# Half-width column sums, earlier decode states, later gate work and a longer last yield in a one-layer hybrid decoder step

## The chip, the core and the metric

The kernel runs on one core of one Trainium2 chip. A core has the matrix engine TensorE (PE), whose weight loads are listed apart as PEld, the vector engine VectorE (DVE), the scalar engine ScalarE (ACT), GpSimd (POOL), and SyncE (SP), which issues most of the DMAs. Each engine works through its own instructions in order and waits on semaphores for the others. The metric is the device time of one execution in microseconds (us), as the median of several runs.

## What is computed

One inference step of a one-layer decoder, for a prompt of 1024 positions and for 8 decode sequences of 4 positions, width 1024, all in float32. Two half-step feed-forward layers stand around a mixer of two groups of heads: a matrix-memory recurrence (mLSTM, 4 heads of 128) and sliding-window attention (SWA, 8 heads of 64).

```python
def half_ffn(x, j, gpre, gpost):
    y = swiglu(rmsnorm(x, g[gpre]), ffn_w_gate[l, j], ffn_w_up[l, j], ffn_w_down[l, j])
    return x + 0.5 * rmsnorm(y, g[gpost])

x = half_ffn(x, 0, 0, 1)
h = rmsnorm(x, g[2])
(qm, km, vm, om, ip, fp), (qa, ka, va) = split_proj(h, w_in[l], b_gate[l])
u_m, new_m = mlstm_heads(qm, km, vm, om, ip, fp, mstate, mlstm_norm_gain[l], h.dtype)
u_a, new_kv = swa_prompt(qa, ka, va, attn_sinks[l])      # swa_sample for the decode rows
u = jnp.concatenate([u_m, u_a], axis=-1)
x = x + rmsnorm(u @ w_out[l], g[3])
x = half_ffn(x, 1, 4, 5)
```

```python
def rmsnorm(x, g):
    y = xf * lax.rsqrt(jnp.mean(xf * xf, axis=-1, keepdims=True) + RMS_EPS)
    return (y * g.astype(jnp.float32)).astype(x.dtype)

def mlstm_chunk(carry, xs):                              # state C, n, m; gates ig, fg
    b = jnp.cumsum(jax.nn.log_sigmoid(fg), axis=-1)
    ...
    m_t = jnp.maximum(inter, jnp.max(D, axis=-1))        # running maximum
    num = a[..., None] * jnp.einsum('bhtk,bhkv->bhtv', q, C) + jnp.einsum('bhts,bhsv->bhtv', S, v)
    ...
    C_new = decay[..., None, None] * C + jnp.einsum('bhs,bhsk,bhsv->bhkv', wk, k, v)
```

The outputs are the new x of both parts, the last keys and values, and the new states C, n, m.

## The kernel before

The 1056 rows (1024 of the prompt, 32 of the decode sequences) are held transposed, features on the partitions, in four quarters of 264 columns (`QW`): 256 of the prompt and 8 of decode. Two blocks of 128 features, `kp` pairs, lie side by side in a tile of 128x528. Each float32 weight is split by ACT (`wh`, a cast, L196) and DVE (`wl`, the rest, L197), activations likewise, and a product is three matmuls (`wh` by high, `wl` by high, `wh` by low), all recorded at the line of the helper `pe`, L154.

There are three phases: 1 is the first feed-forward layer, 2 the mixer's output projection, 3 the second feed-forward layer. In a feed-forward layer `gu` are the gate and up matmuls and `pd` the down matmuls; in the mixer `pz` is the input projection and `po` the output projection.

**What sets the order.** The Python program emits instructions for all engines in one pass. `Order` keeps a clock `now`, advanced by an estimate for every matmul that `pe` emits. Side work is written as generators: `yield w` puts the rest of the generator off until `now` has moved on by `w` us of planned PE time. What is emitted between two yields goes into each engine's queue at that place, SP's DMAs and POOL's copies too; the engine keeps this order on the chip.

**After a product block** (`post`). `out_block` takes a `ps` of `pd` or `po` to the tile `y` and its square into `acc`, summed on DVE (L502). `col_stats` sums squares over the partitions with matmuls against a column of ones: for three windows of 128 columns (`WIN`, of which the third overlaps the second) and the two halves of the tile, six one-column matmuls into `cs`. `rstd` makes the reciprocal root of it on DVE (L260 to L271), a matmul (`rb`) spreads it over the partitions, ACT copies it (`cr`), DVE scales `y` (L443) and adds the residual `x` (L444). Where another layer follows, the new rows are squared (ACT L448), summed (DVE L452) and go through `col_stats` again. `post` yields `PW[0]` = 4.0 before the first sums and `PW[3]` = 6.0 before the second. Phase 3 ends with `store_y`: `yT`, transposes on PE (L151), copies (`yo`) and stores.

**The last quarter** has a class of its own, `Last`. `block(mo, ps)` runs for each of the eight row blocks `mo`; `first` and `second` turn `y` as it comes. `finish` computes the sums from two tiles, `acc[0]` (row blocks 0 to 6) and `acc[1]` (the last, squared at L545), with six matmuls, then scales and stores (L590 to L596).

**Gates** (`gate_rows`, `gates`). The gate rows are turned by PE into `gr`, copied by ACT to `H` and `lf` (L966), scanned by DVE (L992: four cumulative sums and then four running maxima for each of two groups), and then exponentials are formed by ACT into `G` (L996, L998, L999). Beside that runs attention: scores `sws`, their exponentials (ACT L1102), transposes `swp` on PE, a copy of these to `swpT` by ACT (L1136) or DVE (L1138), and the product `swo` on PE.

**Decode states** (`mlstm_sample`). For the 8 decode sequences, in pairs: load the state `Cb` (128x4x128; SP L1436), copy in the column of `n` (POOL L1437), 8 matmuls `sinter` of the queries with the old state, 8 matmuls `sU` of keys and values, DVE updates of the state (L1455), and the store `o_s_C` (SP L1460). Between the parts stand yields of `BW` = 2.4. The loads of a pair come right ahead of its matmuls. The weight loads of `w_out` (SP L1602, L1604) are on the same queue and wait until a raw buffer (`NRAW` = 2) has been read.

## Time and profile before

| | us |
|---|---|
| three runs of the kernel | 2036.6, 2038.76, 2040.52 |
| their median | 2038.76 |
| profiled execution, its own time | 2040.95 |
| span of its profile | 2039.1 |
| granted TensorE clock, mean | 0.988 |
| TensorE busy | 2007.4 |
| VectorE, ScalarE, GpSimd busy | 1165.4, 873.8, 34.1 |

The span runs from the first to the last instruction of the profile; the profiled execution took 1.85 us more. Busy shares are of the span. An arrow `<-` in a row joins what is written to what is read; behind the bar of a row of a group stand its busy time, the mean time of one in ns, and the idle time of the engine just ahead with what ended it. In a row of the timeline or the chain the first two numbers are the start and the length in us, and the square bracket is the idle time just ahead with its releaser. A matmul of float32 operands, as in `cs`, leaves two records, so the x12 of a chain piece are six matmuls.

### The profile page before, as it was taken

What the parts mean: (1) busy time and instruction counts of PE and PEld (TensorE: products, weight loads), DVE (VectorE), ACT (ScalarE), POOL (GpSimd) and SP (SyncE); (2) the same over time, 40 slices, a digit from 0 to 9 for tenths busy, and PEclk for the clock granted to TensorE, in tenths of its full rate; (3) what the DMA queues carried; (4) which work ended last, traced back from release to release, by engine and by line L of the source; (5) the groups of instructions that cost most, each with busy time, mean ns of one, the idle gap of its engine ahead of it and who ended that gap; (6) DMA issues with size and microseconds to landing.
All of it is one profiled execution on the core that took longest, in us unless ns stands there. A gap on an engine that the chain in (4) does not pass through costs nothing.

```text
span 2039.1 us, 40481 instructions
## 1 busy us (share of the span) xinstructions
PE 2007.4 (98%) x16244; PEld 1962.1 (96%) x16244; DVE 1165.4 (57%) x2811; ACT 873.8 (43%) x2087; POOL 34.1 (2%) x166
## 2 busy tenths in 40 slices
PE   7999999999999999999999999999999999999998
PEld 7999999999999999987998999999999999999998
DVE  6855555557248236467455757785555556533764
ACT  6533333336246232356252555353333334433553
POOL 0000000000000002000001000000000000000000
PEclk9999999999999999999998999999999999999999
DMA  6122222236256252101313234322222223544773
GB/s 234 65 81 87 83 64 83 85 100 176 87 161 203 86 147 87 49 1 38 75 52 101 75 108 134 117 64 90 68 75 82 89 70 118 166 132 153 215 233 115
DMA packets 279691, 216.68 MB, mean 106 GB/s; under 512 B 21032, under 2 KB 252640, under 8 KB 279488
## 3 DMA queue, kind: packets, MB, share of 16 engines
q1 hardware_dynamic: 279504, 214.11, 34.7%
q8 instruction: 127, 2.08, 0.4%
q14 instruction: 60, 0.49, 0.1%
HBM read 172.39 MB, written 42.49 MB: 105 GB/s over the span
## 4 chain that ended last, share of the span: by engine, by line
PE 91%; DMA 3%; DVE 3%; ACT 1%; issue 1%; SPq 0%; DVEq 0%; POOL 0%; ACTq 0%; POOLq 0%
PE gu L154 40%; PE pd L154 23%; PE pz L154 7%; PE pw L154 4%; PE pl L154 4%; PE pv L154 3%; PE po L154 3%; DMA raw<-ffn_w_down 2%; PE cs L154 1%; PE sws L154 1%; PE swo L154 1%; PE rb L154 1%; PE E L154 1%; PE swp L151 1%; ACT wh L196 0%
## 5 line engine op out<-in xcount | busy, mean ns | idle before, releaser
L154 PE MATMUL gu<-Xh,wh 128*128 128x264 f32 x2240 | 636.1, 284 | 1.2 <-ACT sc L736 1.2
L154 PE MATMUL gu<-Xl,wh 128*128 128x264 f32 x2240 | 636.2, 284 | 0.0
L154 PE MATMUL gu<-Xh,wl 128*128 128x264 f32 x2240 | 635.8, 284 | 0.0
L197 DVE TENSOR_TENSOR wl<-raw,wh 128x512 fp32r<-128x512 f32 x458 | 302.5, 670 | 390.4 <-ACT wh L196 383.6
L154 PE MATMUL pd<-hq,wh 128*128 128x264 f32 x2816 | 523.1, 287 | 0.0
L196 ACT CAST wh<-raw 128x512 fp32r<-128x512 f32 x458 | 270.5, 602 | 468.1 <-PE pd L154 200.3
L154 PEld LDWEIGHTS pd<-hq,wh 128*128 128x128 f32 x2816 | 439.4, 190 | 0.0
L154 PEld LDWEIGHTS gu<-Xh,wh 128*128 128x128 f32 x2240 | 421.3, 188 | 1.7 <-ACT sc L736 1.4
L154 PEld LDWEIGHTS gu<-Xh,wl 128*128 128x128 f32 x2240 | 421.6, 188 | 0.0
L154 PEld LDWEIGHTS gu<-Xl,wh 128*128 128x128 f32 x2240 | 421.3, 188 | 0.0
L154 PE MATMUL pd<-hq,wl 128*128 128x264 f32 x1408 | 401.7, 285 | 0.0
L154 PEld LDWEIGHTS pd<-hq,wl 128*128 128x128 f32 x1408 | 266.3, 189 | 0.0
L736 ACT COPY sc<-gu 128x264 f32<-128x264 f32 x240 | 90.8, 379 | 273.7 <-PE gu L154 270.6
L197 DVE TENSOR_TENSOR wl<-ws,wh 128x512 fp32r<-128x512 f32 x160 | 108.9, 690 | 87.3 <-ACT wh L196 84.4
L747 DVE TENSOR_TENSOR h<-gu,sc 128x264 f32<-128x264 f32 x120 | 51.8, 432 | 103.2 <-PE gu L154 83.4
L154 PE MATMUL pz<-xh,wh 128*128 128x264 f32 x352 | 103.5, 294 | 0.0
L154 PE MATMUL pz<-xl,wh 128*128 128x264 f32 x352 | 101.9, 289 | 0.0
L154 PE MATMUL pz<-xh,wl 128*128 128x264 f32 x352 | 101.2, 287 | 0.0
L196 ACT CAST wh<-ws 128x512 fp32r<-128x512 f32 x160 | 95.8, 622 | 3.7 <-PE pl L154 2.5
L748 ACT ACTIVATE h<-h 128x264 f32<-128x264 f32 x120 | 50.9, 425 | 106.7 <-DVE h L747 106.7
L753 DVE TENSOR_TENSOR sc<-gu,sc 128x264 f32<-128x264 f32 x120 | 51.6, 432 | 57.2 <-PE gu L154 51.6
L154 PE MATMUL pl<-Xl,wh 128*128 128x264 f32 x256 | 75.3, 298 | 1.0 <-DVE Xl L197 0.8
(367 smaller groups left out, 2997.0 us busy)
## 6 DMA issues: line engine op xcount, KB each, us to landing
raw<-ffn_w_down SPq DMA_DIRECT2D x80, 512.0 KB
raw<-ffn_w_gate SPq DMA_DIRECT2D x44, 512.0 KB
raw<-ffn_w_up SPq DMA_DIRECT2D x44, 512.0 KB
h<-h SPq DMA_DIRECT2D x80, 264.0 KB
hq<-h SPq DMA_DIRECT2D x160, 132.0 KB
raw<-ffn_w_down SPq DMA_DIRECT2D x40, 384.0 KB
x<-xs SPq DMA_DIRECT2D x48, 264.0 KB
raw<-w_in SPq DMA_DIRECT2D x21, 512.0 KB
```

The source lines that it names most:

```text
L151: K.nc.tensor.transpose(out, lhsT, rhs)
L154: K.nc.tensor.matmul(out, lhsT, rhs, start=start, stop=stop, **kw)
L196: K.nc.scalar.copy(hi, src)
L197: (eng or K.nc.vector).tensor_tensor(lo, src, hi.bitcast(F32), op=ALU.subtract)
L736: nc.scalar.copy(sc[n][:, g], ps)
L747: nc.vector.tensor_tensor(d, bk[tg, g], sc[n][:, g], op=ALU.add)
L748: nc.scalar.activation(d, d, AF.Silu)
L753: nc.vector.tensor_tensor(sc[n][:, g], src, sc[n][:, g], op=ALU.add)
```

## The change

Five edits:

1. `col_stats` gets the phase. In phases 1 and 3 DVE first adds the two halves of the sum tile (128x264, in place), and three matmuls follow in place of six. Phase 2 is as before.
2. In the last quarter the three sums of `acc[0]` are made in a task of their own, due 2.0 us after row block 6; the three of `acc[1]` remain in `finish`, and both write one `cs`.
3. In phase 3, `post` yields 2.0 once more before `store_y`.
4. `gate_rows` yields 1.5, 1.5 and 2.0 around its arithmetic, and `gates` yields 7.0 ahead of its exponentials.
5. `mlstm_sample` issues the loads of the first four states (and the POOL copies of their columns) at its start, and later those of the pair after the next.

```diff
@@ -235,12 +235,17 @@
         K.od.tick()
 
 
-def col_stats(K, acc):
+def col_stats(K, acc, phase):
 
     ps = sbank(K, "cs")
+    n = 2
+    if phase != 2:
+
+        K.nc.vector.tensor_tensor(acc[:, 0:QW], acc[:, 0:QW], acc[:, QW:2 * QW], op=ALU.add)
+        n = 1
     for j, w in enumerate(WIN):
-        for i in range(2):
-            pe(K, ps[:, j:j + 1], acc[:, i * QW + w:i * QW + w + P], K.ones, start=(i == 0), stop=(i == 1))
+        for i in range(n):
+            pe(K, ps[:, j:j + 1], acc[:, i * QW + w:i * QW + w + P], K.ones, start=(i == 0), stop=(i == n - 1))
     return ps[:, 0:3]
 
 
@@ -430,7 +435,7 @@
         nc.sync.dma_start(t, K.xs[q][kp])
         x.append(t)
     yield PW[0]
-    ss = col_stats(K, acc.pop())
+    ss = col_stats(K, acc.pop(), phase)
 
     c = rstd(K, ss, 4.0 / D, 4.0 * EPS) if half else rstd(K, ss)
     yield PW[1]
@@ -461,11 +466,12 @@
                 nc.vector.scalar_tensor_tensor(lo, y[kp][:, s], gk, hi.bitcast(F32), op0=ALU.mult, op1=ALU.subtract)
         yield PW[2] if q > 1 else PL[phase]
     if not nxt:
+        yield 2.0
         yield from store_y(K, q, y)
         return
     K.od.done.add(("x", phase, q))
     yield PW[3]
-    r = rstd(K, col_stats(K, acc))
+    r = rstd(K, col_stats(K, acc, phase))
     yield PW[4]
     if nxt == "mix":
         rc = K.kp.tile([P, 3], F32, tag=f"rc{q}", name=nm(K, "rc"), bufs=1)
@@ -548,10 +554,22 @@
         else:
             self.acc.append(sq)
         nc.scalar.activation(y, ps, AF.Copy, scale=gain)
+        if mo == 6:
+            K.od.spawn(self.stats(0), 2.0)
         if mo == 3:
             K.od.spawn(self.first(self.t), 3.0)
         elif mo > 3:
             K.od.spawn(self.second(mo, y), 3.0)
+
+    def stats(self, i):
+
+        if i == 0:
+            self.ss = sbank(self.K, "cs")
+        for j, w in enumerate(WIN):
+
+            pe(self.K, self.ss[:, j:j + 1], self.acc[i][:, w:w + P], self.K.ones, start=(i == j == 0),
+               stop=(i == 1 and j == 2), skip_group_check=True)
+        yield 0
 
     def first(self, t):
         K = self.K
@@ -576,13 +594,11 @@
 
     def finish(self):
         K, q = self.K, self.q
-        ps = sbank(K, "cs")
-        for j, w in enumerate(WIN):
-            for i, sq in enumerate(self.acc):
-                pe(K, ps[:, j:j + 1], sq[:, w:w + P], K.ones, start=(i == 0), stop=(i == 1))
+        for _ in self.stats(1):
+            pass
         K.od.drain()
 
-        c = rstd(K, ps[:, 0:3], 4.0 / D, 4.0 * EPS)
+        c = rstd(K, self.ss[:, 0:3], 4.0 / D, 4.0 * EPS)
         for j in range(3):
             for x in range(2):
                 o = tmp(K, "yo", 512)
@@ -946,12 +962,15 @@
     nc.gpsimd.tensor_copy(R[:, :, 0:4], v[:, :, 0:4])
     nc.scalar.activation(e, f, AF.Abs)
     nc.scalar.activation(e, e, AF.Exp, scale=-1.0)
+    yield 1.5
 
     nc.vector.tensor_scalar(u, e, 1.0, None, op0=ALU.add)
     nc.vector.scalar_tensor_tensor(d, u, 1.0, e, op0=ALU.subtract, op1=ALU.subtract)
     nc.vector.tensor_scalar(e, e, -0.5, 1.0, op0=ALU.mult, op1=ALU.add)
     nc.vector.tensor_tensor(d, d, e, op=ALU.mult)
+    yield 1.5
     nc.scalar.activation(u, u, AF.Ln)
+    yield 2.0
     nc.vector.tensor_tensor(u, u, d, op=ALU.subtract)
     nc.vector.scalar_tensor_tensor(R[:, :, 32:36], f, 0.0, u, op0=ALU.min, op1=ALU.subtract)
     yield 8.0
@@ -993,6 +1012,7 @@
         nc.vector.tensor_tensor(K.mst[:, c + 1:c + 2], b[:, o + P - 1:o + P], M[:, o + P - 1:o + P], op=ALU.add)
     nc.vector.tensor_scalar(p(I), p(M), -1.0, None, op0=ALU.mult)
     nc.vector.tensor_tensor(p(d), p(b), p(M), op=ALU.add)
+    yield 7.0
     nc.scalar.activation(p(G[64:68]), p(d), AF.Exp, scale=-1.0)
     for c, o in chunks:
         nc.scalar.activation(G[32:36, o:o + P], M[:, o:o + P], AF.Exp, bias=K.mst[:, c:c + 1], scale=-1.0)
@@ -1400,12 +1420,22 @@
 
     nc, A, O = K.nc, K.A, K.O
     c = 8
+    states = []
+
+    def state(b):
+        Cb = slot(K, "Cb")[:, 0:516].rearrange("p (h v) -> p h v", v=129)
+        nc.sync.dma_start(Cb[:, :, 0:P], A["state_mlstm_C"][0, b].rearrange("h k v -> k h v"))
+        nc.gpsimd.tensor_copy(Cb[:, :, P], n0[:, b])
+        states.append(Cb)
+
     nrow = tmp(K, "n0", P)[0:32]
     nc.sync.dma_start(nrow, A["state_mlstm_n"][0].rearrange("b h k -> (b h) k"))
     ps = bank(K, "n0T", "c")
     pe(K, ps[:, 0:32], nrow, K.ident[0:32, 0:32], tr=True)
     n0 = K.kp.tile([P, 8, 4], F32, tag="n0", name="n0", bufs=1)
     nc.vector.tensor_copy(n0.rearrange("p b h -> p (b h)"), ps[:, 0:32])
+    for b in range(4):
+        state(b)
     E = scores(K, c, [K.sz[:, 6 + h] for h in range(HM)], [K.sz[:, 10 + h] for h in range(HM)], K.H[2][0], 32, slot)
 
     kr = slot(K, "kr")[:, 0:512]
@@ -1430,12 +1460,10 @@
     nn = K.kp.tile([P, 8, 4], F32, tag="nn", name="nn", bufs=1)
     for b0 in range(0, 8, 2):
 
-        bs, C = (b0, b0 + 1), []
-        for b in bs:
-            Cb = slot(K, "Cb")[:, 0:516].rearrange("p (h v) -> p h v", v=129)
-            nc.sync.dma_start(Cb[:, :, 0:P], A["state_mlstm_C"][0, b].rearrange("h k v -> k h v"))
-            nc.gpsimd.tensor_copy(Cb[:, :, P], n0[:, b])
-            C.append(Cb)
+        bs = (b0, b0 + 1)
+        for b in range(len(states), min(b0 + 4, 8)):
+            state(b)
+        C = [states[b] for b in bs]
         for b, Cb in zip(bs, C):
             for h in range(HM):
                 q = qm[h // 2][:, (h % 2) * 256 + b * 32:(h % 2) * 256 + b * 32 + 32]
```

Three places where the order of the instructions moves. Numbers behind a name count tiles as the program makes them, and the same tile has another number in the changed kernel; its line numbers are shifted too.

SP, at the decode states (`raw` a buffer for `w_out` weights, `Cb` a state to be loaded, `o_s_C` the output of new states), before:

```order
L1602 DMA raw_13850<-w_out 128x4x128
L1604 DMA raw_13850<-w_out 64x4x128 x2
L1602 DMA raw_14144<-w_out 128x4x128
L1604 DMA raw_14144<-w_out 64x4x128 x2
L1436 DMA Cb_13686<-state_mlstm_C 128x4x128
L1436 DMA Cb_13689<-state_mlstm_C 128x4x128
L1436 DMA Cb_13751<-state_mlstm_C 128x4x128
L1436 DMA Cb_13754<-state_mlstm_C 128x4x128
L1460 DMA o_s_C<-Cb_13686 128x4x128
L1460 DMA o_s_C<-Cb_13689 128x4x128
L1460 DMA o_s_C<-Cb_13751 128x4x128
L1460 DMA o_s_C<-Cb_13754 128x4x128
```

SP at the same place after the change, where L1602, L1604, L1436 and L1460 are L1630, L1632, L1427 and L1488:

```order
L1630 DMA raw_13840<-w_out 128x4x128
L1632 DMA raw_13840<-w_out 64x4x128 x2
L1427 DMA Cb_13619<-state_mlstm_C 128x4x128
L1427 DMA Cb_13622<-state_mlstm_C 128x4x128
L1427 DMA Cb_13625<-state_mlstm_C 128x4x128
L1427 DMA Cb_13628<-state_mlstm_C 128x4x128
L1630 DMA raw_14128<-w_out 128x4x128
L1632 DMA raw_14128<-w_out 64x4x128 x2
L1488 DMA o_s_C<-Cb_13619 128x4x128
L1488 DMA o_s_C<-Cb_13622 128x4x128
L1427 DMA Cb_13741<-state_mlstm_C 128x4x128
L1427 DMA Cb_13744<-state_mlstm_C 128x4x128
```

The four state loads have moved ahead of the second `w_out` load; the loads of the third pair stand behind two stores, where before they stood behind the four that are shown.

ACT, at the gates of the first group (`H`, `lf` and `G` of the gates; `sws`, `es`, `swpT`, `kT` of attention), before:

```order
L1102 ACTIVATE sws_11477,den_11473<-sws_11477,nmx_11472 128x256 x2
L966 COPY H_11551<-gr_11546 4x2x256
L966 COPY lf_11552<-gr_11546 4x2x256
L998 ACTIVATE G_11556<-lf_11552,mst 4x128 x4
L1136 COPY swpT_11641<-swp_11636 128x512
L999 ACTIVATE G_11556<-G_11556,H_11551 4x128 x3
L996 ACTIVATE G_11556<-gb_11555 4x2x256
L999 ACTIVATE G_11556<-G_11556,H_11551 4x128
L1119 COPY kT_11676<-kT_11674 128x128
```

ACT after the change, from the same `swpT` copy on (L1136, L1102, L1099, L966 are L1156, L1122, L1119, L985):

```order
L1156 COPY swpT_11592<-swp_11587 128x512
L1119 ACTIVATE es_11539<-es_11539 128x4
L1122 ACTIVATE sws_11544,den_11541<-sws_11544,nmx_11540 128x256 x2
L1122 ACTIVATE sws_11545,den_11541<-sws_11545,nmx_11540 128x256 x2
L985 COPY H_11617<-gr_11612 4x2x256
L985 COPY lf_11618<-gr_11612 4x2x256
```

ACT after the change, the rows that follow directly (`z` takes up `swo`, `wh` is a weight cast, L998 is L1018):

```order
L1170 COPY z_9873<-swo_11502 128x128
L1139 COPY kT_11651<-kT_11649 128x128
L1170 COPY z_9937<-swo_11502 128x128
L1018 ACTIVATE G_11622<-lf_11618,mst 4x128 x2
L196 CAST wh_11785<-raw_11783 128x512
L1018 ACTIVATE G_11622<-lf_11618,mst 4x128
L1156 COPY swpT_11707<-swp_11702 128x512
L1018 ACTIVATE G_11622<-lf_11618,mst 4x128
```

The `swpT` copy that stood behind the four instructions of L998 now stands ahead of the copies to `H` and `lf`, and the next `swpT` copy stands behind three of the four.

DVE, at the third set of sums in phase 1 (`wl` a weight rest, `sq` squares, `xl` the rest of an activation), before:

```order
L197 TENSOR_TENSOR wl_8253<-raw_8250,wh_8252 128x512
L444 TENSOR_TENSOR y_7562<-y_7562,x_7844 128x528
L197 TENSOR_TENSOR wl_8257<-raw_8250,wh_8256 128x512
L452 TENSOR_TENSOR sq_8014<-sq_8014,sq_8219 128x528
L461 SCALAR_TENSOR_TENSOR xl_1257_8165<-y_7562,gain,xh_1256_8164 128x264
L461 SCALAR_TENSOR_TENSOR xl_1259_8169<-y_7562,gain,xh_1258_8168 128x264
L260 TENSOR_SCALAR v_8306<-cs_8299 128x3
L197 TENSOR_TENSOR wl_8332<-raw_8329,wh_8331 128x512
```

DVE at the same place after the change, where L452, L461, L260 are L457, L466, L265 and L244 is the new add:

```order
L197 TENSOR_TENSOR wl_8249<-raw_8246,wh_8248 128x512
L197 TENSOR_TENSOR wl_8253<-raw_8246,wh_8252 128x512
L457 TENSOR_TENSOR sq_8031<-sq_8031,sq_8221 128x528
L466 SCALAR_TENSOR_TENSOR xl_1255_8153<-y_7562,gain,xh_1254_8152 128x264
L466 SCALAR_TENSOR_TENSOR xl_1257_8157<-y_7562,gain,xh_1256_8156 128x264
L244 TENSOR_TENSOR sq_7943<-sq_7943 128x264
L197 TENSOR_TENSOR wl_8326<-raw_8323,wh_8325 128x512
L265 TENSOR_SCALAR v_8303<-cs_8298 128x3
L197 TENSOR_TENSOR wl_8330<-raw_8323,wh_8329 128x512
```

The new add of the halves stands behind the last accumulation and two `xl` rows of another quarter, and ahead of the first operation of `rstd` that reads `cs`.

## Prediction

> **What bounds the kernel now.** I read the page first: how busy each engine is, the granted clock over the span, and by engine the chain of work that ended last.

> ```profile
> span 2039.1 us, 40481 instructions
> PE 2007.4 (98%) x16244; PEld 1962.1 (96%) x16244; DVE 1165.4 (57%) x2811; ACT 873.8 (43%) x2087; POOL 34.1 (2%) x166
> PEclk9999999999999999999998999999999999999999
> PE 91%; DMA 3%; DVE 3%; ACT 1%; issue 1%; SPq 0%; DVEq 0%; POOL 0%; ACTq 0%; POOLq 0%
> ```

> TensorE (PE) is busy 98% of the span, and 91% of the chain is PE. So time can go in three ways only: fewer matmuls, less of the 31.7 us (2039.1 − 2007.4) in which PE idles, or fewer microseconds at a lower clock. The idle time and the clock dips are few, so I cut the span into stages and read PE's busy time and the clock of each; the columns are the stretch, its length, the busy time of each engine, then clock, DMA share and GB/s.

> ```profile
> core 0: us, PE busy (x) PEld busy (x) DVE busy (x) ACT busy (x) POOL busy (x), PEclk, DMA share, GB/s
> 625.00:750.00 125.00, 125.00 (x1032) 125.00 (x1031) 57.48 (x129) 47.89 (x102) 0.00 (x0) 1.00 0.41 116
> 850.00:950.00 100.00, 97.13 (x727) 79.03 (x727) 68.81 (x317) 55.93 (x192) 1.73 (x6) 0.97 0.09 23
> 1100.00:1130.00 30.00, 27.54 (x185) 21.89 (x183) 13.97 (x38) 8.53 (x14) 4.32 (x21) 0.66 0.50 141
> 1950.00:2000.00 50.00, 47.11 (x376) 46.21 (x375) 29.42 (x57) 26.52 (x55) 0.00 (x0) 0.97 0.68 203
> ```

> The first row is typical of the feed-forward layers: PE without a gap at full clock. The others hold what the change can touch: 2.9 us of idle before 950, 2.5 in the decode stretch with a clock of 0.66, 2.9 in 1950–2000. Finer cuts show where the clock is halved:

> ```profile
> 939.20:946.00 6.80, 6.80 (x34) 5.55 (x31) 3.82 (x25) 3.60 (x15) 0.00 (x0) 0.50 0.05 12
> 1106.40:1109.80 3.40, 2.60 (x22) 1.62 (x22) 0.61 (x2) 0.00 (x0) 0.00 (x0) 0.50 0.50 139
> 1120.10:1123.50 3.40, 3.40 (x20) 3.17 (x19) 0.00 (x0) 0.18 (x1) 0.00 (x0) 0.50 0.99 273
> 1123.50:1126.90 3.40, 3.40 (x19) 3.16 (x22) 1.12 (x2) 3.37 (x4) 0.00 (x0) 0.50 0.60 164
> 1126.90:1130.30 3.40, 3.40 (x38) 2.27 (x34) 2.78 (x10) 0.28 (x1) 0.38 (x2) 1.00 0.34 97
> 1881.20:1884.60 3.40, 3.40 (x17) 3.40 (x18) 1.65 (x12) 0.41 (x1) 0.00 (x0) 0.51 0.02 7
> ```

> The clock is 0.5 in stretches that are multiples of about 3.4 us: two units from 939.2 (behind a PE wait of 2.7 us), six from 1106.4 to 1126.9, one at 1881.2. Half clock costs half of its length: 3.4, 10.25 and 1.7 us. At 1881.2 PE had not idled at all; it had run two sets of column sums.

> The idle time by what ended it (total, times, longest):

> ```profile
> PE swo L154 <- ACT swpT L1136: 2.9, 2, 2.7
> PE sinter L154 <- DMA Cb<-state_mlstm_C: 1.9, 1, 1.9
> PE yT L151 <- DVE y L444: 1.7, 1, 1.7
> PE cs L154 <- DVE sq L502: 0.9, 1, 0.9
> ```

> **Column sums (phases 1 and 3).** Each set of six one-column matmuls `cs` becomes one VectorE (DVE) add of 128x264 and three matmuls. In the chain a piece counts two records for a matmul, so x12 is a set of six:

> ```profile
> 625.94 1.23 PE cs L154 x12
> 627.17 3.78 PE pd L154 x30
> ...
> 658.18 1.23 PE cs L154 x12
> ...
> 1878.43 1.23 PE cs L154 x12
> ...
> 1880.14 1.33 PE cs L154 x12
> ...
> 1954.75 1.50 PE cs L154 x12
> ```

> A set costs 1.23 us, with PE work directly behind it; half is 0.615. Eight sets in phase 1 give 4.9 us. In phase 3 the two sets at 1878 give 1.28. The set at 1954.75 saves 0.75, but PE waits there already 0.9 us for the sum that the add now follows, so the add comes on top.

> ```profile
> L747 DVE TENSOR_TENSOR h<-gu,sc 128x264 f32<-128x264 f32 x120 | 51.8, 432 | 103.2 <-PE gu L154 83.4
> L197 DVE TENSOR_TENSOR wl<-raw,wh 128x512 fp32r<-128x512 f32 x458 | 302.5, 670 | 390.4 <-ACT wh L196 383.6
> ```

> No row of before adds the halves of one tile. The nearest row of that size takes 432 ns, the one of 128x512 670; I take 0.43 us. At 1954.75 that leaves −0.3. Elsewhere the add is free where it ends before PE reaches the sums. The last accumulation stands 2.8 us ahead of the set at 625.94 (the timeline of VectorE has it at 621.74 with 1.36 us for two):

> ```profile
> 621.74 1.36 DVE L502 TENSOR_TENSOR sq<-sq,sq 128x528 f32<-128x528 f32 x2
> ...
> 658.42 0.89 DVE L461 SCALAR_TENSOR_TENSOR xl<-y,gain,xh 128x264 fp32r<-128x264 f32 x2
> ```

> But VectorE is in order, and behind it the add waits for what is queued ahead. At the third set (658.18 in before) the add stands behind the two L461 operations that end at 659.31. With PE and VectorE both about 1 us earlier by then, and the set 11 matmuls later in PE's order, I expect a wait of 0.5 us (between 0 and 1.4). Sum: −4.9 − 1.3 − 0.3 + 0.5 = **−6.0 us**; the ends are −6.5 (add hidden everywhere) and 0 (each add late by what its matmuls saved). The half-clock unit at 1881.2 follows 2.6 us of sums within 3.2; single sets of 1.23 us cost no clock in phase 1 (clock 1.00 in 625–750). With 1.3 us of sums in that place the unit should stay at full clock: **−1.7** (ends 0 and −1.7).

> **Decode states.** Now the first four state loads stand ahead of a `w_out` load on the DMA-issuing queue (SP), which is held until a raw buffer is read:

> ```profile
> 1094.72 1.41 SPq L1604 DMA_DIRECT2D raw<-w_out  x2
> 1100.70 0.37 SPq L1602 DMA_DIRECT2D raw<-w_out  x1
> ...
> 1102.42 3.31 SPq L1436 DMA_DIRECT2D Cb<-state_mlstm_C  x4
> ```

> From their issue to PE's release takes 4.8 us (1102.42 to 1107.20). They no longer stand behind the load of 1100.70, and can issue behind the `w_out` load that ends its issue at 1096.13 (1094.72 + 1.41). With the same 4.8 us they land near 1101; PE stood waiting from 1105.3 in before and wants them at about 1104 now. The 1.9 us wait goes. Late next is the load of the third pair: it stands behind the first pair's two state stores, which wait for VectorE's updates. Its price lies between 0 and the 1.9 us of the wait that was; PE has 15 dense `po` matmuls to cover it (1.9 us at full clock, by the 3.78 us of 30 `pd` above), and I take 0. The moved `w_out` load comes at most four issues (3.31 us) later and feeds a cast 15 us on; four POOL copies now stand ahead of the copy of the keys, which so comes 0.64 us later:

> ```profile
> 1116.15 0.62 ACT L196 CAST wh<-raw 128x512 fp32r<-128x512 f32 x1 [12.05 <-PE po L154]
> ...
> 1101.30 0.32 POOL L1437 COPY Cb<-n 128x4 f32<-128x4 f32 x2
> ```

> The cast waited for PE, not for the load, and VectorE reads the keys after a microsecond of planned PE work: 0 for both, at most 0.6.

> What matters more is the clock. PE's order now runs the first two pairs' 32 small matmuls in one block, then twice 15 `po` and a pair. In before such small matmuls, mixed with `po`, kept PE busy without restoring the clock:

> ```profile
> 1119.04 2.18 PE sU L154 x16
> 1121.22 5.58 PE po L154 x24
> ```

> The clock came back at 1126.9 only, after a unit of `po` alone; the unit 1120.1–1123.5, two thirds `po`, brought nothing. Fifteen `po` at half clock last 15/24 of 5.58 = 3.5 us, one unit, which would have to fall on the grid exactly; so I take the halved stretch as starting and ending about where it did: cost 0, ends −8.5 (one unit instead of six) and +3.4 (two more). Term: **−1.9**.

> [...]

> **Gates.** The ScalarE (ACT) work of the gates is issued later, past attention work. In before:

> ```profile
> 934.08 0.40 ACT L998 ACTIVATE G<-lf,mst 4x128 f32<-4x128 f32 x1 [3.58 <-DVE lf L992]
> 935.21 0.40 ACT L998 ACTIVATE G<-lf,mst 4x128 f32<-4x128 f32 x1 [0.73 <-DVE lf L992]
> ...
> 936.77 0.40 ACT L998 ACTIVATE G<-lf,mst 4x128 f32<-4x128 f32 x1 [0.47 <-DVE lf L992]
> 937.20 0.58 ACT L1136 COPY swpT<-swp 128x512 f32<-128x512 f32 x1
> ```

> The `swpT` copy that PE waits for stood behind four Exps, each held by a VectorE scan. In the new order that copy goes ahead of them, but the next `swpT` stands behind three of them. Laying the new order out with these durations, I get that copy ending near 942.8 and PE there from 940.4 to 941.1: again 1.7 to 2.4 us of wait, with smaller ones beside it. So the wait moves and the two half-clock units with it: **0**, ends −6.1 (2.7 of wait and 3.4 of clock gone) and +3.4 (two more units).

> **End of the last quarter.** The transposes `yT` of quarter 2 come about 17 dense matmuls later behind their row broadcast (2.1 us), past the wait for DVE's `y`: **−1.7**, ends 0 and −1.7, since VectorE itself waits there for a weight load. At the very end three of six sums go ahead into the matmul stream: 0.6 us less behind the last square, 0.6 more PE work before it: **0**.

> **Sum:** −6.0 − 1.7 − 1.9 + 0 − 1.7 + 0 = −11.3 us. The profiled execution took 2040.95 us; this gives 2029.7. It is 2.2 us above the median of the three runs (2038.76), against which the forecast is 2027.5.

> **Rivals.**
> 1. The decode clock returns early, or hardly falls. For it: the state wait that opened the stretch is gone, and 15 `po` are nearly a whole unit. Against: the unit two thirds full that did not restore. Price 8.5 us: 2019. Chance 0.20.
> 2. The gates' wait goes, and the clock stays up there: 6.1 us more: 2021.5. For it: one `swpT` is freed. Against: the three Exps ahead of the next. Chance 0.10.
> 3. The waits only move, and are paid twice: the third pair's load is late (1.9) and the small matmuls hold the clock down two units longer (3.4), or the gates cost two units more (3.4): 5 to 7 us less gain, 2032.5 to 2034.5, and together with late adds within 0.2% of before. Chance 0.16.
> 4. Slower: the adds, queued behind VectorE's weight splits, come late at the sums. A set gains while its wait is under 0.615 us. A wait of one split (0.67 us) plus the add (0.43) costs 1.1 − 0.6 = 0.5 for a set, 5.5 for 11 in place of a gain of 6; with a half-clock unit of 1.7 us behind each it is 2.2 × 11 = +24 in place of −6, and the total 2057. The other terms give −5.3, so the point from which this decides is 5.3 + 4.1 = 9.4 us of loss, 0.9 a set or waits of 1.5 us. Against it: of the eleven sets, I find only the third and the one at 1954.75 with VectorE that close behind. Chance 0.04.

> **Numbers.** Forecast 0.50 (its own range 2024 to 2031). From the cases: faster by over 0.2% (4.1 us, about what a measurement of this kernel can tell from no change) 0.50 + 0.20 + 0.10 + 0.07 of the third = 0.87; within 0.2% 0.09; slower 0.04. The range reaches down past the first rival (2016) and up to the third (2034); some 0.15 is left out.

> **What would show it.** Right: `cs` records halved in phases 1 and 3 with no PE wait behind the adds beyond 0.5 us at the third set; clock 1.00 where 1881.2 was; no wait of `sinter` for the state load; about 20 us of half clock still in the decode stretch; the `swo` wait still about 2 us but on a later copy; no `yT` wait for `y`. Wrong: waits of `cs` on the adds in several places, more half-clock units than before, or a decode stretch with one or two.

## The result and the profile after

The changed kernel takes 2018.93 us (median of 4 runs, 2016.99 to 2019.93) against 2038.63 us before (4 runs, 2036.6 to 2040.52): a ratio of 0.9902, 95% interval 0.9885 to 0.992. That is 19.7 us or 1% faster, inside the predicted range and on the mark of its first rival (2019), well below the forecast of 2027.5. By a threshold of 2% the two count as the same; by the 0.2% of the prediction the change is faster.

The head of the page after the change, in the same order as before (span, busy time by engine, granted clock over the span, chain by engine):

```profile
span 2017.4 us, 40347 instructions
PE 1986.5 (98%) x16178; PEld 1942.6 (96%) x16178; DVE 1168.4 (58%) x2822; ACT 874.9 (43%) x2087; POOL 35.6 (2%) x166
PEclk9999999999999999999999999999999999999999
PE 91%; DVE 3%; DMA 3%; ACT 2%; issue 1%; SPq 0%; DVEq 0%; ACTq 0%
```

The span fell by 21.7 us. PE's idle time explains next to nothing of it: 31.7 us before, 30.9 now (2017.4 − 1986.5). PE's busy time fell by 20.9, and the windows of the changed kernel tell why (columns as before):

```profile
625.00:750.00 125.00, 123.45 (x1002) 123.19 (x1001) 58.13 (x131) 47.89 (x102) 0.00 (x0) 0.99 0.41 115
850.00:950.00 100.00, 98.41 (x759) 80.43 (x759) 71.40 (x325) 58.87 (x202) 2.11 (x8) 1.00 0.06 17
1090.00:1130.00 40.00, 39.05 (x371) 33.59 (x371) 26.91 (x82) 18.14 (x39) 6.19 (x25) 1.00 0.51 140
1230.00:1335.00 105.00, 103.83 (x826) 102.48 (x825) 89.45 (x209) 50.20 (x102) 0.00 (x0) 0.97 0.28 93
1870.00:1905.00 35.00, 34.31 (x287) 33.70 (x286) 24.39 (x41) 16.68 (x35) 0.00 (x0) 1.00 0.68 212
1940.00:1990.00 50.00, 48.16 (x397) 46.95 (x396) 28.90 (x49) 26.88 (x56) 0.00 (x0) 1.00 0.59 177
```

The decode stretch (1090–1130) and the gates (850–950) are at clock 1.00 throughout, and so are the places of the units near 1881 and 1956. Counted in units of 3.4 us, each of which costs by estimate 1.7 where PE is busy throughout (half its length, at clock 0.50), before had twelve while PE still had work: two behind the gates, six at the decode states, two at the end of phase 2 (1307.8), one at 1881.2, one at 1956.3. The changed kernel has three: one from 633.1 (called the one near 632 below) and two from 1288.5. Nine units are 15.4 us by that estimate, a little less where PE idled in them. The rest, 21.7 − 15.4 − 0.8 = 5.5 us, is a remainder and not a measurement; the halved sums can account for it, since 33 one-column matmuls fewer, at 1.23 us for six, are 6.8 us of PE work.

Within the traces of before and of the changed kernel the half-clock stretches, and the distances between them, are whole numbers of 3.41 us (of before: from 946.0 to 1106.4 are 47 units; of the changed kernel: from 633.1 to 1288.5 are 192). These points are called the grid here.

The waits of PE in the changed kernel:

```profile
PE swo L154 <- ACT swpT L1156: 1.6, 3, 1.0
PE yT L151 <- DVE y L449: 1.6, 2, 0.9
PE rb L154 <- DVE v L265: 1.5, 1, 1.5
PE cs L154 <- DVE sq L244: 0.8, 1, 0.8
PE sinter L154 <- DMA Cb<-state_mlstm_C: 0.6, 1, 0.6
```

The state wait went from 1.9 to 0.6 us and the longest `swpT` wait from 2.7 to 1.0. The wait for `y` is as long as before, in two pieces. A new one of 1.5 us, of `rb` at 632.8, has the half-clock unit behind it: VectorE's root (from 632.60) stood there behind a weight split (from 631.65), whose cast on ScalarE had waited 2.80 us for the load.

So most of the gain is clock. The experiments ask which edit brought it, and what the clock goes by.

### The profile page after: what moved, and what is told of

It is laid out like the page before. It is cut to its first block, busy times and chain, and to the rows that moved or that the text cites. A ratio compares the mean times of both kernels' runs of the same rounds, so it can differ in the third digit from the quotient of the medians.

```text
span 2017.4 us, 40347 instructions
## 1 busy us (share of the span) xinstructions
PE 1986.5 (98%) x16178; PEld 1942.6 (96%) x16178; DVE 1168.4 (58%) x2822; ACT 874.9 (43%) x2087; POOL 35.6 (2%) x166
## 4 chain that ended last, share of the span: by engine, by line
PE 91%; DVE 3%; DMA 3%; ACT 2%; issue 1%; SPq 0%; DVEq 0%; ACTq 0%
PE gu L154 41%; PE pd L154 23%; PE pz L154 7%; PE pw L154 4%; PE pl L154 4%; PE pv L154 3%; PE po L154 2%; DMA raw<-ffn_w_down 2%; PE cs L154 1%; PE rb L154 1%; PE swo L154 1%; PE sws L154 1%; PE E L154 1%; ACT wh L196 1%; PE swp L151 1%
## 5 line engine op out<-in xcount | busy, mean ns | idle before, releaser
L154 PE MATMUL gu<-Xh,wh 128*128 128x264 f32 x2240 | 636.6, 284 | 0.0
L154 PE MATMUL gu<-Xl,wh 128*128 128x264 f32 x2240 | 636.0, 284 | 0.0
L154 PE MATMUL gu<-Xh,wl 128*128 128x264 f32 x2240 | 635.1, 284 | 0.0
L197 DVE TENSOR_TENSOR wl<-raw,wh 128x512 fp32r<-128x512 f32 x458 | 301.6, 670 | 384.3 <-ACT wh L196 376.5
L154 PE MATMUL pd<-hq,wh 128*128 128x264 f32 x2816 | 520.8, 286 | 0.1
L196 ACT CAST wh<-raw 128x512 fp32r<-128x512 f32 x458 | 270.1, 602 | 459.4 <-PE pd L154 193.2
L154 PEld LDWEIGHTS pd<-hq,wh 128*128 128x128 f32 x2816 | 437.8, 189 | 0.4 <-ACT yo L853 0.4
L154 PEld LDWEIGHTS gu<-Xh,wh 128*128 128x128 f32 x2240 | 421.1, 188 | 0.5 <-ACT sc L752 0.2
L154 PEld LDWEIGHTS gu<-Xh,wl 128*128 128x128 f32 x2240 | 421.6, 188 | 0.0
L154 PEld LDWEIGHTS gu<-Xl,wh 128*128 128x128 f32 x2240 | 421.3, 188 | 0.0
L154 PE MATMUL pd<-hq,wl 128*128 128x264 f32 x1408 | 401.1, 285 | 0.0
L154 PEld LDWEIGHTS pd<-hq,wl 128*128 128x128 f32 x1408 | 265.4, 188 | 0.2 <-DVE wl L197 0.2
L197 DVE TENSOR_TENSOR wl<-ws,wh 128x512 fp32r<-128x512 f32 x160 | 108.8, 690 | 87.6 <-ACT wh L196 84.7
L763 DVE TENSOR_TENSOR h<-gu,sc 128x264 f32<-128x264 f32 x120 | 51.8, 432 | 102.2 <-PE gu L154 83.3
L154 PE MATMUL pz<-xh,wh 128*128 128x264 f32 x352 | 102.3, 291 | 0.6 <-DVE z L1684 0.6
L154 PE MATMUL pz<-xh,wl 128*128 128x264 f32 x352 | 100.8, 286 | 0.0
L154 PE MATMUL pz<-xl,wh 128*128 128x264 f32 x352 | 100.5, 285 | 0.0
L196 ACT CAST wh<-ws 128x512 fp32r<-128x512 f32 x160 | 95.9, 623 | 4.1 <-PE pl L154 2.5
L154 PE MATMUL pl<-Xh,wh 128*128 128x264 f32 x256 | 72.9, 299 | 3.3 <-ACT Xh L196 2.1
```

The lines of the kernel that those rows point to most:

```text
L154: K.nc.tensor.matmul(out, lhsT, rhs, start=start, stop=stop, **kw)
L196: K.nc.scalar.copy(hi, src)
L197: (eng or K.nc.vector).tensor_tensor(lo, src, hi.bitcast(F32), op=ALU.subtract)
L763: nc.vector.tensor_tensor(d, bk[tg, g], sc[n][:, g], op=ALU.add)
```

## The experiments

Each ratio below is to the kernel before on the same chip; its interval is about 0.0017 to either side, so a difference of two ratios is known to about 5 us. The profiles tell the rest, each for one execution.

The mean granted clock is known for every run, also for those without a profile. One minus it, times the span, estimates the time lost to the clock; the clock is rounded to 0.001, which is 2 us in a single run.

| kernel | runs | mean clock | us lost, estimate |
|---|---|---|---|
| before (three chips) | 45 | 0.989 | 21.6 |
| changed (with `again`) | 8 | 0.996 | 7.9 |
| `u_dec`, `o_dec` | 4, 6 | 0.993, 0.995 | 14.7, 10.8 |
| `u_gates`, `o_gates` | 4, 10 | 0.993, 0.992 | 14.2, 17.1 |
| `u_cs`, `u_end` | 4, 4 | 0.996, 0.995 | 8.6, 9.6 |
| `p_cs4`, `p_wide` | 4, 10 | 0.990, 0.995 | 21.5, 10.2 |

These hold the end of the span too, where PE has no work left and the clock is at half (3.8 us lost so from 2031.4 on in the profile before, 2.6 from 2012.0 on in the one after). So of the 19.7 us about 14 are clock over all runs, in line with the 15.4 of the two profiles. Without the early decode states or without the later gate work 6 to 7 us of clock are lost again; with the full column sums next to none.

### One edit taken back at a time

**`u_dec`**: the changed kernel with the loads of each pair right ahead of its matmuls.

```diff
-    for b in range(4):
-        state(b)
...
-        for b in range(len(states), min(b0 + 4, 8)):
-            state(b)
-        C = [states[b] for b in bs]
+        bs, C = (b0, b0 + 1), []
+        for b in bs:
+            Cb = slot(K, "Cb")[:, 0:516].rearrange("p (h v) -> p h v", v=129)
+            nc.sync.dma_start(Cb[:, :, 0:P], A["state_mlstm_C"][0, b].rearrange("h k v -> k h v"))
```

> The changed kernel with the decode states loaded as before (each pair right ahead of its matmuls). Theory: the 1.9 us wait for the state load is what halved the clock, and the six half-clock units behind it (10.2 us) hang on it; so with the wait back, 10 to 13 us are lost again: 2029 to 2032 us, with a wait of sinter for the load of about 2 us and several half-clock units behind it. Rival (the term as it was forecast): only the wait comes back, about 2 us: 2021, the clock being held or lost there by the small matmuls in any case. Second rival: the clock dip hung on the grid of the units and comes back only by chance: no difference in the clock, 2021.

Measured: 2027.75 us, ratio 0.995 (0.9934 to 0.9966), so 0.0048 or 9.8 us are lost again, a little less than the 10 to 13 expected. PE waits 1.6 us for the first states. The windows of this kernel, cut on the grid:

```profile
1094.38:1097.79 3.41, 1.62 (x19) 1.22 (x17) 3.18 (x6) 0.98 (x2) 0.00 (x0) 1.00 1.00 247
1097.79:1101.20 3.41, 3.10 (x23) 2.12 (x24) 0.99 (x4) 0.00 (x0) 0.00 (x0) 0.50 0.51 124
1101.20:1104.61 3.41, 3.41 (x13) 2.55 (x11) 1.26 (x5) 0.00 (x0) 0.38 (x2) 0.50 0.48 142
...
1111.44:1114.85 3.41, 3.41 (x19) 3.19 (x16) 0.41 (x1) 0.62 (x1) 0.00 (x0) 0.50 1.01 281
1114.85:1118.26 3.41, 3.41 (x35) 2.60 (x35) 1.95 (x7) 3.21 (x3) 0.00 (x0) 1.00 0.54 156
```

In the first unit PE is busy for 1.62 us of 3.41; the next is at half clock, and five are in all (8.5 us by estimate, half their length), though PE idles in only the first of the five. The changed kernel runs the same kinds of matmuls there at full clock (here the whole unit on its grid that holds small matmuls alone, and the one behind it):

```profile
1097.35:1100.76 3.41, 3.41 (x63) 2.77 (x62) 3.41 (x11) 0.00 (x0) 0.52 (x2) 1.00 0.03 7
1100.76:1104.17 3.41, 3.27 (x29) 2.82 (x27) 3.27 (x11) 0.62 (x1) 1.16 (x7) 1.00 0.97 266
```

The small matmuls alone, a whole unit of them, did not bring the clock down here; a unit that was about half busy (1.62 of 3.41 us) did, in `u_dec`. So the first theory holds for the long dip, and the forecast term (the dip stays) falls. `d_one` below shows a single unit of half clock that came without such a wait.

**`o_dec`**: the kernel before with that edit alone.

> The kernel before with the early decode states alone. Theory: the state wait (1.9 us) goes and with it most of the six half-clock units (10.2 us): 10 to 12 us faster than before, 2025 to 2029 us, clock 1.00 or one or two units in the decode stretch, the two units behind the gates as in before. Rival (the forecast term): only the wait goes, 2 us faster, the clock still halved for about 20 us.

Measured: 2027.07 us, ratio 0.9959 (0.9945 to 0.9972), 8.4 us faster than before where 10 to 12 were expected, and no half-clock unit in the decode stretch. Its trace holds a surprise at the gates, whose order is that of before:

```profile
PE swo L154 <- ACT swpT L1136: 2.9, 2, 2.7
PE sinter L154 <- DMA Cb<-state_mlstm_C: 1.6, 2, 1.0
```

The same 2.7 us wait as before, and no half-clock unit behind it in this execution. The grid tells the two apart. The first row is the unit of before that holds most of the wait, the two behind it are those of `o_dec` over which it falls:

```profile
935.75:939.16 3.41, 1.32 (x13) 0.82 (x14) 3.28 (x14) 2.71 (x7) 0.00 (x0) 1.00 0.00 0
```

```profile
933.35:936.76 3.41, 1.92 (x15) 1.58 (x14) 3.05 (x12) 1.20 (x3) 0.19 (x1) 1.00 0.00 0
936.76:940.17 3.41, 2.24 (x19) 1.29 (x19) 2.88 (x14) 3.18 (x9) 0.00 (x0) 1.00 0.00 0
```

In before PE is left with 1.32 us of work in one unit; in `o_dec` an edge of the grid cuts the wait in two, and the units have 1.92 and 2.24. Two state waits of up to 1.0 us brought no half clock here either. A sharp border in busy time can't be read from the traces: a unit with 1.59 us busy was not followed by half clock (`u_end`, 1945.7), one with 2.67 was (`u_cs`, 1109.8).

**`u_gates`**: the changed kernel without the yields in `gate_rows` and `gates`.

```diff
-    yield 1.5
...
-    yield 1.5
     nc.scalar.activation(u, u, AF.Ln)
-    yield 2.0
...
-    yield 7.0
     nc.scalar.activation(p(G[64:68]), p(d), AF.Exp, scale=-1.0)
```

> The changed kernel with the four yields around the gates' arithmetic and exponentials taken out. Theory: PE waits again over 2 us in one piece for the swpT copy behind four exponentials, and two half-clock units follow: +1.3 of wait and +3.4 of clock, 2023 to 2025 us. Rival (the term as it was forecast): the wait only moves, within 1 us of the changed kernel, 2018 to 2020.

Measured: 2024.08 us, ratio 0.9933 (0.9916 to 0.995), 6.3 us more than the changed kernel, with the uncertainty of 5. Its longest `swpT` wait and the window behind it:

```profile
PE swo L154 <- ACT swpT L1152: 2.9, 2, 2.6
```

```profile
932.80:943.10 10.30, 9.29 (x43) 7.07 (x44) 6.14 (x34) 6.03 (x20) 0.00 (x0) 0.54 0.02 6
```

Three units at half clock here, two in before, none in `o_dec`, for the same wait of 2.6 to 2.7 us. The theory holds, but a wait's price in clock is not fixed. The four runs agree with the trace: a mean clock of 0.993 in each, against 0.995 to 0.997 in the eight of the changed kernel.

**`o_gates`**: the kernel before with that edit alone.

> The kernel before with the later gate work alone. Theory: the longest swpT wait falls from 2.7 to about 1 us and the two half-clock units behind it go: 5 to 6 us faster than before, 2031 to 2034 us, with the decode stretch at half clock as in before. Rival (the forecast term): the wait moves, no difference to before.

Measured: 2033.87 us, ratio 0.9978 (0.9966 to 0.9991), 4.5 us faster, a little short of the 5 to 6 expected. No unit at the gates, five at the decode states behind a state wait of 2.0 us.

**`u_cs`**: six sums and no add in all phases.

```diff
-    if phase != 2:
+    if phase > 9:
```

> The changed kernel with six column-sum matmuls and no add in all phases. Theory: the eight sets of phase 1 and two of phase 3 cost 0.6 us each again (+6), and the pair of sets at the start of the last stage halves the clock for one unit (+1.7): 2025 to 2028 us. If the 1.5 us wait of rb and the half-clock unit near 632 of the changed kernel came from the shorter sums, 3.2 us of that are given back: 2022 to 2025. Rival: the sums lay beside other work and cost nothing, 2018 to 2020.

Measured: 2022.99 us, ratio 0.9928 (0.9914 to 0.9943): 5.3 us more with the uncertainty of 5, in line with the remainder of 5.5 us read above, and with a clock that is not lower (a mean of 0.996 in both). Neither the wait of `rb` near 632 nor its unit is there; one half-clock unit stands in the decode stretch (1113.2). But no unit stands at the two sets at the start of the last stage either, where the theory put one.

**`u_end`**: without the extra yield and with all sums of the last quarter in `finish`.

```diff
     if not nxt:
-        yield 2.0
         yield from store_y(K, q, y)
...
-        if mo == 6:
-            K.od.spawn(self.stats(0), 2.0)
```

> The changed kernel without the extra yield ahead of the last stores and with all six sums of the last quarter at the end. Theory: the wait of the transposes for y is a little longer again and the half-clock unit near 1956 of before may come back: +0.5 to +3.5, 2019.5 to 2022.5 us; the sums of the last quarter change the place of 0.6 us of PE work only. Rival: both cost nothing, 2018 to 2020, and the unit near 1956 was removed by the halved sums.

Measured: 2019.78 us (2016.6 to 2023.47), ratio 0.9911 (0.9893 to 0.993), 1.8 us more with an uncertainty of 5. What this part is worth stays open. The four parts taken back add up to 23.2 us, over the 19.7 of the whole; the uncertainties allow that, and the parts need not be independent.

### What the clock goes by

**`again`**: the changed kernel, in another execution.

> The changed kernel itself, unaltered, to see it in another execution and on the chip of the next three. Theory (the units lie on a free grid, so that the same waits lower the clock in one execution and not in another): the time as before, 2016 to 2021 us, but half-clock units of the trace in other places or of another number than 1 near 632 and 2 near 1290; the decode stretch at full clock or nearly. Rival (the units belong to the kernel): the same units in the same places.

Measured: 2018.69 us, ratio 0.9899 (0.9881 to 0.9917). Two windows of this trace:

```profile
1230.00:1335.00 105.00, 103.57 (x843) 102.19 (x842) 91.28 (x213) 51.84 (x106) 0.00 (x0) 1.00 0.28 93
1930.00:1940.00 10.00, 9.34 (x65) 9.34 (x66) 6.46 (x20) 4.14 (x9) 0.00 (x0) 0.83 0.73 223
```

The two units at the end of phase 2 are missing, the one near 632 as well (its wait of 1.5 us is there), and one has appeared near 1932. So the same program has other units in another execution. At the end of phase 2 PE's wait for the sums and the sums themselves last as long in both (0.42 and 1.47 us). In the profile above both lie within one unit, which ends at 1288.5; in `again` an edge of the grid (1287.2, counted back from 1932.3) cuts the sums. So the grid lies differently in the two executions, and that is the likely reason for the two units.

The unit near 1932 has another cause. It stands behind the sums of the third quarter in phase 3, where the new add is late. That set in the profile above, then in `again`:

```profile
1933.72 0.83 PE L154 MATMUL cs<-ones,sq 128*128 128x1 f32 x6 [0.84 <-DVE sq L244]
```

```profile
1930.66 0.83 PE L154 MATMUL cs<-ones,sq 128*128 128x1 f32 x6 [1.59 <-DVE sq L244]
```

Of the nine traces with the add at this set, `again` is the usual one: PE waits 1.6 to 1.8 us in seven and 2.8 in `v_all`, and a half-clock unit follows in seven. The profile shown above (0.8 us, no unit) is the mildest. With six sums and no add there the wait was 0 to 0.9 us in five traces (`before`, `o_dec`, `o_gates`, `u_cs`, `v_sel`).

**`p_cs4`**: every column sum of phase 1 made four times.

```diff
         for i in range(n):
-            pe(K, ps[:, j:j + 1], ..., K.ones, start=(i == 0), stop=(i == n - 1))
+            for _ in range(4 if phase == 1 else 1):
+                pe(K, ps[:, j:j + 1], ..., K.ones, start=(i == 0), stop=(i == n - 1))
```

> The changed kernel with every column sum of phase 1 made four times over: 12 matmuls of one column in a row, 2.46 us, at each of eight places, none of them with an idle PE. It computes the same values. Theory (the clock gate counts a PE busy with one-column matmuls as idle): beside the 1.85 us of PE work at each place (14.8 us) several of the eight places are followed by a half-clock unit of 1.7 us: 2036 to 2046 us, and the half clock shows in windows in which PE is fully busy. Rival (only an idle PE lowers the clock): 14.8 us and no half-clock unit in phase 1 beyond that of the changed kernel, 2033 to 2035.

**`p_wide`**: the same, each matmul against 64 columns of ones.

```diff
+    K.wide = K.cp.tile([P, 64], F32, tag="wide", name="wide")
...
+                    pe(K, ps[:, 64 * j:64 * j + 64], ..., K.wide, start=(i == 0), stop=(i == n - 1))
```

> As the kernel with every column sum of phase 1 made four times, but each matmul against 64 columns of ones in place of one, of which the first is used. It computes the same values. Theory (the clock gate counts the columns that stream through the array, and not whether PE is busy): PE's time for the sums grows a little (0.2 to 0.4 us per matmul), but phase 1 keeps the full clock or loses one or two units where the one-column sums lost seven: 2030 to 2042 us in all. Rival (the gate counts something else, such as weight loads or gaps between matmuls): six to eight units as there, 2045 to 2060 us.

Measured: `p_cs4` 2048.75 us, ratio 1.0064 (1.0049 to 1.0079), above the 2036 to 2046 of its theory; `p_wide` 2038.42 us, ratio 1.0001 (0.9989 to 1.0014), within the range of its theory. The first set in the chain of `p_cs4`, then in that of `p_wide`:

```profile
626.34 2.57 PE cs L154 x24
```

```profile
624.92 2.62 PE cs L156 x24
```

PE is busy for nearly the same time with one column or 64 (2.57 and 2.62 us for twelve matmuls); no run shows the 0.2 to 0.4 us more per matmul that the theory of `p_wide` had put. Windows of `p_cs4` at its first two sets, and of `p_wide` at its own:

```profile
625.60:629.00 3.40, 3.40 (x33) 3.40 (x32) 0.73 (x2) 1.14 (x2) 0.00 (x0) 1.00 1.04 356
629.00:632.40 3.40, 3.40 (x18) 3.40 (x18) 2.23 (x12) 0.62 (x1) 0.00 (x0) 0.52 0.62 185
632.40:635.80 3.40, 3.40 (x31) 3.40 (x31) 0.99 (x2) 0.41 (x1) 0.00 (x0) 0.98 0.19 48
635.80:639.20 3.40, 3.40 (x19) 3.40 (x18) 1.31 (x8) 0.00 (x0) 0.00 (x0) 0.52 0.44 131
```

```profile
624.90:627.50 2.60, 2.60 (x26) 2.60 (x25) 0.94 (x2) 1.14 (x2) 0.00 (x0) 1.00 0.98 330
627.50:630.90 3.40, 3.40 (x30) 3.40 (x30) 2.13 (x12) 0.89 (x2) 0.00 (x0) 1.00 0.84 243
```

In `p_cs4` PE shows 3.40 of 3.40 us busy, and the unit after the sums is at half clock; phase 1 has seven such units (12 us by estimate, half their length). `p_wide` has none. By their ratios the two differ by 12.8 us, and the mean clock is 0.989 to 0.991 in the four runs of `p_cs4`, 0.992 to 0.997 in the ten of `p_wide`. So in these two traces a PE that is busy with one-column matmuls counts as idle, or nearly so, for the clock (seven units); 64 columns in the same time count as work (none). Weight loads do not decide it here: both kernels have 192 records of them for these sums, of the same shape (128x128).

### Other depths and more halved sums

**`d_one`**: only the first pair of states early.

```diff
-    for b in range(4):
+    for b in range(2):
         state(b)
...
-        for b in range(len(states), min(b0 + 4, 8)):
+        for b in range(len(states), min(b0 + 2, 8)):
```

> The changed kernel with only the first pair of decode states loaded early, the other pairs right ahead of their matmuls. Theory: only the wait that PE meets ahead of the first pair's matmuls sets the clock down; PE's order has 27 po matmuls ahead of the second pair's, which cover its load, so the time is that of the changed kernel, 2016 to 2021 us. Rival (two pairs ahead are needed): waits for the second or third pair of 1 to 2 us and the clock down behind them, 2022 to 2030 us.

Measured: 2021.98 us, ratio 0.9924 (0.9901 to 0.9948), beside 0.9899 of the changed kernel on the same chip: unclear, the intervals overlap. PE does not wait for a state in it, so the second pair need not be early for that. One half-clock unit (1100.7) stands in the decode stretch all the same:

```profile
1097.30:1100.71 3.41, 3.41 (x22) 2.64 (x20) 2.99 (x9) 0.00 (x0) 2.12 (x8) 1.00 0.44 127
1100.71:1104.13 3.42, 3.42 (x16) 3.23 (x16) 0.62 (x1) 0.62 (x1) 0.02 (x1) 0.50 1.06 281
```

By the records PE does not idle in the unit ahead of it, which mixes small matmuls with a few `po`. So one unit of half clock followed such a mix here; why, and why not in the changed kernel, is not shown. Over all traces, the decode stretch has six or five units where the first pair is loaded late (before, `u_dec`, `o_gates`). Where it is early, it has none in eight traces and one in three (`u_cs`, `d_one`, `v_all`).

**`v_all`**: the halved sums in phase 2 too.

```diff
-    if phase != 2:
+    if phase:
```

> The changed kernel with the halved column sums in phase 2 too. Theory: eight more sets save 0.6 us of PE each, but in phase 2 VectorE sets the end of several sets (PE waits for the last accumulation at the last quarter already), so that the add comes on top there: between -5 and +2 against the changed kernel, most likely -3, 2014 to 2018 us; the half-clock units near 1290, which follow 1.0 us of waits and 1.5 us of sums, shrink or go if sums count as idle. Rival: VectorE is the bound in phase 2 and the adds cost what they save, 2018 to 2022 us.

Measured: 2022.84 us, ratio 0.9938 (0.992 to 0.9957), some 7 us slower than the changed kernel (uncertainty 5) and above both of the ranges expected. Its waits:

```profile
PE cs L154 <- DVE sq L244: 5.1, 3, 2.8
PE rb L154 <- DVE r L276: 3.0, 3, 2.3
```

At the last quarter of phase 2 (1.8 us) and the third of phase 3 (2.8), PE waits for the add. It is the mechanism of the slower rival, in the places where VectorE sets the pace; the second place has the add in the changed kernel too.

**`v_sel`**: the halved sums also for the first two quarters of phase 2, and not for the third quarter of phase 3.

```diff
-    if phase != 2:
+    if (phase, q > 1) not in ((2, True), (3, True)):
```

> The changed kernel with the halved sums also in phase 2 for the first two quarters, and without them for the third quarter of phase 3, where PE waits for the add. Theory: four more sets save 0.6 us each beside free VectorE time, and the set of phase 3 changes little: 2 to 3 us faster than the changed kernel, 2015 to 2018 us. Rival: the adds are late there as in the last quarter, no gain or a loss, 2018 to 2023 us.

Measured: 2032.65 us, ratio 0.997 (0.9956 to 0.9983), 14 us slower than the changed kernel and far outside both of the ranges expected. The longest wait in the timeline of its PE, and the window around it:

```profile
1290.88 1.42 PE L154 MATMUL rb<-ident,r 128*128 128x128 f32 x6 [6.66 <-DVE r L276]
```

```profile
1230.00:1300.00 70.00, 60.47 (x459) 59.26 (x458) 51.05 (x137) 25.54 (x52) 0.00 (x0) 0.88 0.33 112
```

PE waits 6.7 us at the end of phase 2 for a root of a later quarter, whose sums were not changed, and five units at half clock lie around it. The matmuls left out shorten the planned time, and with it everything that is placed by yields moves; this is the likely cause, but it wasn't tried by itself. A version faster than the changed kernel was not found. Sums against a wider block of ones in phases 2 and 3, which `p_wide` suggests, were not tried.

## Why the prediction was right in its range and wrong in its forecast

- **Bound**: right. PE is still busy 98%, and the time went by the three ways named; two of them did the work, clock (15.4 us in the profiles, about 14 over all runs) and matmuls (some 6).
- **Column sums, −6.0**: right in size as far as can be told; a remainder of 5.5 us in the trace, 5.3 (uncertainty 5) when taken back. The 0.5 us wait at the third set did not come. At the set of the last stage the prediction put one add, 0.43 us, on top of the 0.9 us wait. The profile of the changed kernel shows 0.8 us in all, but that was luck: `again` waits 1.59, with a half-clock unit behind it, so that most of the 0.75 us that the halved set saves there is lost again.
- **The unit at 1881, −1.7**: it is gone, and that sums count as idle, or nearly so, is what `p_cs4` shows with its seven units. Of the four traces with the full sums there, before and `o_dec` (1868.6, with PE fully busy ahead of it) have such a unit, `u_cs` and `o_gates` have none. So such a unit stood behind the two sets in two traces of four; the gain of 1.7 was not sure.
- **Decode states, −1.9**: the mechanism of the wait was right, the price wrong; taking the edit back costs 9.8 us, alone it brings 8.4. The step that failed reads "I take the halved stretch as starting and ending about where it did". It came from a true observation, that these matmuls did not bring the clock back (20.5 us of half clock in before), and a false turn of it, that they would also hold it down where no wait had opened the dip. `u_dec` beside the changed kernel shows the two apart; what is left of the step is a single unit in three of eleven traces. This was the first rival, given 0.20, and a decode stretch with none is beyond the one or two that the prediction had named as a sign of being wrong.
- **Gates, 0**: wrong. 6.3 us when taken back (uncertainty 5), 4.5 alone (1.8 to 6.9). The step that failed is the layout that put the end of the next `swpT` copy near 942.8 and the wait at 1.7 to 2.4 us: in the timeline of the changed kernel the third exponential starts at 940.20 and the copy ends at 941.21, and PE waited 0.98. The copy of `lf` that the scans wait for ended at 934.71 already. This was the second rival, given 0.10.

```profile
934.13 0.58 ACT L985 COPY lf<-gr 4x512 f32<-4x512 f32 x1
...
940.20 0.40 ACT L1018 ACTIVATE G<-lf,mst 4x128 f32<-4x128 f32 x1
940.62 0.59 ACT L1156 COPY swpT<-swp 128x512 f32<-128x512 f32 x1
```

- **End of the last quarter, −1.7**: not seen as a wait (1.7 before, 1.6 in two pieces now); by time 1.8 with an uncertainty of 5. The sums put ahead, 0, can't be told from it.
- **The whole**: both rivals came true, so that the time agrees with that of the first alone by chance. The forecast with both would be −11.3 − 8.5 − 6.1 = −25.9 us, 2012.9, below the range stated; that the time lay in the range is in part luck. Of the 6.2 us between that and the 19.7, the profiled execution accounts for 4.9: the new wait of `rb` near 632 with its unit (1.5 + 1.7) and the wait for `y` that stayed (1.7). The rivals were priced one at a time, though nothing made them exclude each other.
- **Slower rival**: as a whole it did not happen. Its mechanism did at one of the eleven sets, the one at 1954.75 in before, as `again` and `v_all` show; the prediction had named that set as one where VectorE is close behind.

## What to carry to other kernels

Where a matmul-bound kernel has a dip of the granted clock, look for the wait ahead of it: here a wait of 1.9 us and the dip behind it came to 12 us in the profile and 8 to 10 in time, and the dip, not the wait, is most of what its removal is worth. Price such dips as the first guess when the wait goes, and don't take from the work that fails to restore the clock that it would have lowered it (here five or six units of half clock behind the wait, none or one without it). Count such dips in more than one execution, or by the mean clock of many runs, before pricing them (the changed kernel had three in one execution and one in another). Shortening work that a planner counts moves everything behind it, so a small saving may open a long wait elsewhere.
